# Two pairs of 64x64 products of a DeltaNet scan step, issued together over all four quadrants of the matmul array

## The chip, the cores and the metric

The kernel runs on one core of a Trainium2 chip. The metric is device time in microseconds (us) for one execution: the median of several runs, where lower is better. TensorE is called PE below, its weight loads PEld, VectorE DVE, ScalarE ACT, GpSimd POOL, and SyncE SP; SP issues nearly all DMAs.

## The reference, cut to what matters

One layer of a hybrid block: 2048 latent tokens and 256 context tokens, width 1024, all in float32. One input projection feeds two branches: neighbourhood attention (8 heads of 64, windows of 8 x 16 positions plus all context keys) and a gated DeltaNet that runs over the tokens forwards and backwards (8 heads, keys and values of 64, chunks of 64 tokens). The DeltaNet is computed chunk by chunk:

```python
def step(S, xs):
    qk_i, qd_i, kd_i, u_i, w_i, gt_i = xs
    v_new = u_i - jnp.einsum('bhck,bhkv->bhcv', w_i, S)
    o_i = jnp.einsum('bhck,bhkv->bhcv', qd_i, S) + jnp.einsum('bhij,bhjv->bhiv', qk_i, v_new)
    S = S * gt_i[..., None, None] + jnp.einsum('bhck,bhcv->bhkv', kd_i, v_new)
    return S, o_i
...
o_f, s_f = _gdn_chunked(q, k, v, g[:, :, 0], beta[:, :, 0], s0_f)
o_b, s_b = _gdn_chunked(rev(q), rev(k), rev(v), rev(g[:, :, 1]), rev(beta[:, :, 1]), s0_b)
return o_f + rev(o_b), s_f, s_b
```

Both branches are gated, projected, merged with sigmoid gates, projected once more and added to the input.

## The kernel before

**The stages.** Input projection, the DeltaNet's preparation and its triangular solves come first. Then follows a stage in which two things run woven together: the DeltaNet's scan and the attention. The output projections come last. The change touches the scan and, in three small places, the attention.

**The scan.** There are 36 steps: 4 over the context, then 32 *main* steps. A step treats one forward chunk and one backward chunk at once: direction d = 0 has partitions 0 to 63 of every tile, d = 1 has partitions 64 to 127. The state `sd` is 128 x (8 heads x 64). `scan_step` (L854) has four products, each of 16 matmuls (8 heads, 2 directions) of 64 x 64 by 64 x 64; a float32 matmul shows as two records, so a product is a batch of 32 records. Here they are called **k** (L866, keys times state, z = 0), **q** (L866, queries times state, z = 1), **p2** (L882, the chunk's solved matrix times the residual), **p4** (L889, growth of the state) and **p3** (L896, the output). That is five batches in a main step, three in a context step. Direction 0 reads and writes the lower halves of its tiles and direction 1 the upper halves, so of the array's four 64x64 quadrants the two on the diagonal are used.

The evictions: DVE multiplies k by a decay into tile `cr` (L868), subtracts that from `cv` (L871), multiplies q by the same decay into `cr` (L868 again); ACT copies p2 to `cw` (L884); DVE adds p4 to the state (L890) and subtracts p3 from the q part to give the output `co` (L898). The PSUM pool `pc` has two buffers, taken in turn.

In main steps 0 to 15 the output is stored to `os_` (L901) for the later step that treats the same chunks in the other direction. In main steps 16 to 31 the output is complete, and one step later `dn_out` (L910) normalises it: a square on ACT, a sum on DVE, a power on POOL (`ro`, L917), a product on DVE (L918), four transposes into a `pc` buffer (L922), and an eviction by DVE (`zd`, L923).

**The attention.** 32 units of 128 queries and 4 heads, handled as two pairs of heads. `scores` (L1063) and `scores_ctx` (L1063 too) form the logits; DVE adds a bias table to them (L1073) and finds the maxima (L1080, L1082); ACT takes the exponentials of the window part (L1085) and of the context part (L1088). `turn` (L1096) transposes the window part of the two heads into two tiles of the two-buffer PSUM pool `ptp`: DVE copies the first out and ACT the second (L1098, `pT`). `turn_ctx` (L1105) transposes the context part into the next `ptp` buffer, that is, the one that `turn`'s first tile held. `values` (L1116, L1120) applies the weights, `sums_inv` (`ri`, L1124 to L1128) inverts the sums, `finish` (L1133 to L1139) scales. Units at the grid's edges read the bias from the single-buffer tiles `tedge`, loaded in `att_load` (L1031); inner units read `tmid`.

**The order.** PE's order is written out by hand (`manual_schedule`, L978). The scan is a generator, and each `pump(chain, 1)` runs it to its next yield; a main step has seven yields and a unit seven pumps, so one step goes with one unit:

```python
pump(chain, 1)        # k
un.turn()
pump(chain, 1)        # q
un.turn_ctx(0)
un.scores(1)
pump(chain, 1)        # p2
...                   # scores_ctx(1), sums_inv, values(0)
pump(chain, 2)        # dn_out's transposes, then p4
un.turn()
pump(chain, 1)        # p3
un.turn_ctx(1)
...                   # scores(0) of the next unit, values(1), scores_ctx(0), finish
```

The orders of the other engines and of SP's queue are not written in the kernel: a scheduler (`schedule_with_timeline_sim`) settles them when the program is built.

One line outside this stage is of use below: L623, in the DeltaNet's preparation, multiplies keys and queries of two chunks with 64x64 matmuls in all four quadrants: first 16 records in the two quadrants that write partitions 0 to 63, then 16 in the two that write 64 to 127.

Of the kernel before, what the change touches and what calls it, by code (L numbers as in the profile page):

```python
# [8 lines left out]
F32 = mybir.dt.float32  # L9
F32R = mybir.dt.float32r  # L10
AF = mybir.ActivationFunctionType
ALU = mybir.AluOpType
# [7 lines left out]
P = 128  # L20
# [7 lines left out]
H = 8  # L28
C = 64
NCH = NT // C  # L30
CCH = TC // C
# [54 lines left out]
def body(ctx, tc, x, c, ctx_in, c_ctx, mod_w, mod_b, norm_w, w_in, conv_w, na_q_norm, na_k_norm, na_rpb,  # L86
# [99 lines left out]
    def dn_tokens(d, t0, m):  # L186
        v = d.rearrange("q (n s t) -> q n s t", s=2, t=C)
        c0, n = t0 // C, m // C
        if c0 >= 16:
            return v[:, c0 - 16:c0 - 16 + n, 0]  # L190
        return v[:, 16 - c0 - n:16 - c0, 1][:, ::-1]


    def gate_col(kind, i, p):
# [154 lines left out]
    with ExitStack() as st:  # L349
# [33 lines left out]
        for t in range(0, NTILE, 8):  # L383
            pn = bps.tile([P, 8, 64], F32, name="pn", bufs=2)
            r = range(t, min(t + 8, NTILE))
# [411 lines left out]
    with ExitStack() as st:  # L797
# [56 lines left out]
        def scan_step(i):  # L854

            main = i >= CCH
            ld = scan_in.pop(i)
            scan_load(i + 1)
            eg = egs[:, i].unsqueeze(2).to_broadcast([P, H, C])
            half = [slice(C * d, C * d + C) for d in range(2)]  # L860

            def times_state(z):
                ps = pc.tile([P, H, C], F32, name="pc")
                for h in range(H):
                    for d in range(2):
                        PE.matmul(ps[half[d], h, :], ld["ckq"][half[d], ho(h), z, :], sd[half[d], h, :], start=True, stop=True)  # L866
                t = q2.tile([P, H, C], F32, name="cr")
                V.tensor_tensor(out=t, in0=ps, in1=eg, op=ALU.mult)  # L868
                return t
            r = ld["cv"]  # L870
            V.tensor_tensor(out=r, in0=r, in1=times_state(0), op=ALU.subtract)  # L871
            yield
            if main:
                tq = times_state(1)
                if i - CCH >= 16:
                    G.tensor_tensor(out=tq.rearrange("p h e -> p (h e)"), in0=tq.rearrange("p h e -> p (h e)"), in1=os_[:, NCH - 1 - i], op=ALU.add)
                yield
            G.tensor_tensor(out=sd, in0=sd, in1=gts[:, i].unsqueeze(2).to_broadcast([P, H, C]), op=ALU.mult)  # L878
            p2 = pc.tile([P, H, C], F32, name="pc")
            for h in range(H):  # L880
                for d in range(2):
                    PE.matmul(p2[half[d], h, :], ld["cT"][half[d], ho(h), :], r[half[d], h, :], start=True, stop=True)  # L882
            w = q2.tile([P, H, C], F32, name="cw")
            S.copy(w, p2)  # L884
            yield
            p4 = pc.tile([P, H, C], F32, name="pc")
            for h in range(H):
                for d in range(2):
                    PE.matmul(p4[half[d], h, :], ld["ckd"][half[d], h, :], w[half[d], h, :], start=True, stop=True)  # L889
            V.tensor_tensor(out=sd, in0=sd, in1=p4, op=ALU.add)  # L890
            yield
            if main:
                p3 = pc.tile([P, H, C], F32, name="pc")
                for h in range(H):
                    for d in range(2):
                        PE.matmul(p3[half[d], h, :], ld["cA"][half[d], ho(h), :], w[half[d], h, :], start=True, stop=True)  # L896
                o = q2.tile([P, H, C], F32, name="co", bufs=2)
                V.tensor_tensor(out=o, in0=tq, in1=p3, op=ALU.subtract)  # L898
                if i - CCH < 16:
                    for d in range(2):  # L900
                        SP.dma_start(out=os_[half[d], i - CCH], in_=o[half[1 - d]].rearrange("p h e -> p (h e)"))  # L901
                else:
                    zd = q2.tile([P, 4, P], F32, name="zd", bufs=2)
                    SP.dma_start(out=zd, in_=d_z[1, :, :, P * (i - CCH - 16):P * (i - CCH - 15)].rearrange("p q t -> q p t"))
                    wait.append((i - CCH - 16, o, zd))
# [20 lines left out]
        def scan():  # L926

            for n in range(CCH):
                yield from scan_step(n)
            for n in range(CCH, NCH + 1):  # L930
                dn = dn_out(*wait.pop()) if wait else iter(())
                step = scan_step(n) if n < NCH else iter(())
                next(step, None)
                next(dn, None)
                yield
                for _ in range(2):
                    next(step, None)
                    yield
                next(dn, None)
                yield  # L940
                yield from step
                yield
                yield

        egs = qp.tile([P, NCH, H], F32, name="egs")
        gts = qp.tile([P, NCH, H], F32, name="gts")
        SP.dma_start(out=egs, in_=d_eg)
        SP.dma_start(out=gts, in_=d_gt)
        scan_load(0)
        chain = scan()  # L950
# [66 lines left out]
        def att_load(n):  # L1017
            hg = n // 16
            rg, cg, ty, o, r0, nr, w, br = band(n)
            if cg == 0:  # L1020
                zt = aq.tile([P, 2, 512], F32, name="azt", bufs=2)
                SP.dma_start(out=zt, in_=d_z[0, 2 * hg:2 * hg + 2, :, 512 * rg:512 * rg + 512].rearrange("p q t -> q p t"))
                rg_z[hg, rg] = zt
            if ty == 1:
                tab = [mids[hg][:, 2 * z:2 * z + 2, o:o + nr * w] for z in range(2)]
            elif edge[0] == (hg, rg, o):
                tab = edge[1]
            else:
                tab = [aq.tile([P, 2, 384], F32, name=f"tedge{z}") for z in range(2)]
                for z in range(2):  # L1030
                    SP.dma_start(out=tab[z][:, :, 0:nr * w], in_=d_tab[:, ty, 4 * hg + 2 * z:4 * hg + 2 * z + 2, o:o + nr * w])  # L1031
                edge[:] = (hg, rg, o), tab
            vt = aq.tile([P, 4, 256], F32, name="vt", bufs=2)
            for b in range(nr // br):
                a = TC + 64 * (r0 + br * b)
                SP.dma_start(out=vt[0:br * w, b, :], in_=d_nv[a:a + 64 * br, 256 * hg:256 * hg + 256].rearrange("(r c) e -> r c e", c=64)[:, KEY0[cg]:KEY0[cg] + w, :])
            return tab, vt
# [7 lines left out]
        class Unit:  # L1045
# [76 lines left out]
            def sums_inv(self):  # L1122
                ri = ap.tile([P, 4], F32, name="ri", bufs=2)
                V.tensor_tensor(out=ri, in0=self.sums[:, :, 0], in1=self.sums[:, :, 1], op=ALU.add)  # L1124
                V.tensor_scalar(out=ri, in0=ri, scalar1=2.0, scalar2=None, op0=ALU.mult)
                V.reciprocal(ri, ri)
                self.rb = ap.tile([P, 4, 64], F32, name="rb", bufs=2)
                G.tensor_copy(self.rb, ri.unsqueeze(2).to_broadcast([P, 4, 64]))  # L1128

            def finish(self):  # L1130
# [250 lines left out]
```

## Time and profile before

| what | value |
|---|---|
| median of 3 runs | 2428.86 us (2428.39 to 2434.27) |
| the profiled execution's own time | 2437.24 us |
| its span, first to last instruction | 2435.5 us |
| PE busy | 2208.8 us (91% of the span) |
| PEld busy | 1849.1 us (76%) |
| DVE busy | 1537.0 us (63%) |
| POOL busy | 1064.2 us (44%) |
| ACT busy | 779.9 us (32%) |
| DMA | 358.16 MB, mean 147 GB/s |

The profiled execution took 8.4 us more than the median of the runs; rows of the trace are times from the start of its span. PE's matmuls are pipelined, so records overlap and busy time is not work at its peak; the start of one batch to the start of the next is the better measure. "Idle before <-X" names what ended an engine's wait.

### The profile page before, as it was taken

To read this page: it belongs to the slowest core of one execution; us is meant where nothing else is said; L and a number is where in the kernel's file an instruction comes from. 1 tells how busy PE (TensorE), PEld (TensorE's weight loads), DVE (VectorE), ACT (ScalarE), POOL (GpSimd) and SP (SyncE) were. 2 spreads that over 40 slices of the span, in tenths; PEclk is the share of its full clock that TensorE was granted. 3 is DMA by queue.
4 is the path that set the end of the run, shared out by engine and by line. 5 is a ranking of instruction groups with operands and counts; after the bars stand their busy time and mean duration, and the time that the engine had idled before them with its cause. 6 is when DMAs were issued, how large, how long until landed. Compare 5 with 4: busy or idle time off the path is not lost.

```text
span 2435.5 us, 47134 instructions
## 1 busy us (share of the span) xinstructions
PE 2208.8 (91%) x18323; PEld 1849.1 (76%) x18323; DVE 1537.0 (63%) x2409; ACT 779.9 (32%) x2336; POOL 1064.2 (44%) x856
## 2 busy tenths in 40 slices
PE   6999999988888998998889987989888989899999
PEld 2778777876676787998888766777666767788998
DVE  3736877379959987849849922666566766222222
ACT  4524344211111232343554111444334444211110
POOL 2515677779865211224857510211123324643442
PEclk8999999998998999999999998999999999999999
DMA  7323444665475244254686567777886786544442
GB/s 262 106 70 81 114 118 130 156 152 121 122 173 134 64 88 115 64 131 119 181 200 176 171 153 205 211 195 196 211 216 178 184 195 177 155 118 121 113 115 89
DMA packets 461591, 358.16 MB, mean 147 GB/s; under 512 B 203253, under 2 KB 386697, under 8 KB 460809
## 3 DMA queue, kind: packets, MB, share of 16 engines
q1 hardware_dynamic: 461368, 355.16, 54.7%
q8 instruction: 144, 2.36, 0.4%
q14 instruction: 79, 0.65, 0.1%
HBM read 231.71 MB, written 119.67 MB: 144 GB/s over the span
## 4 chain that ended last, share of the span: by engine, by line
PE 44%; DVE 20%; DMA 12%; POOL 8%; issue 6%; ACT 4%; SPq 3%; DVEq 0%; POOLq 0%; ACTq 0%
PE pd L179 13%; PE pf L1351 7%; PE pu L1340 7%; DVE Xs L579 6%; DVE tmp L577 6%; PE pd L724 5%; PE pw L1063 2%; DMA tedge<-d_tab 2%; ACT pr L1085 2%; PE pc L866 1%; DMA tmk<-in_k_mk_dram 1%; POOL rn L504 1%; PE po L1116 1%; PE pt L1096 1%; DMA d_tab<-tmk 1%
## 5 line engine op out<-in xcount | busy, mean ns | idle before, releaser
L179 PE MATMUL pd<-hT,slots 128*128 128x512 f32 (+1 forms) x3360 | 825.6, 400 | 4.3 <-ACT nx L205 2.5
L179 PEld LDWEIGHTS pd<-hT,slots 128*128 128x128 f32 x3360 | 627.6, 194 | 152.6 <-issue 3.8
L577 DVE TENSOR_TENSOR tmp<-Xs 128x236 f32<-128x236 f32 (+43 forms) x310 | 337.4, 1088 | 62.4 <-DMA Xs<-d_X 54.1
L579 DVE TENSOR_TENSOR Xs<-Xs,tmp 128x236 f32<-128x236 f32 (+43 forms) x310 | 335.8, 1083 | 8.5
L125 POOL TENSOR_TENSOR slots<-w_raw,slots 128x512 fp32r<-128x512 f32 (+1 forms) x76 | 121.0, 1592 | 252.0 <-ACT slots L124 250.2
L724 PE MATMUL pd<-slots,hT 128*128 128x256 f32 x1248 | 165.5, 293 | 0.0
L724 PE MATMUL pd<-wide,hT 128*128 128x256 f32 x1248 | 158.8, 289 | 3.8 <-ACT wide L124 2.6
L724 PEld LDWEIGHTS pd<-slots,hT 128*128 128x128 f32 x1248 | 159.9, 196 | 0.0
L724 PEld LDWEIGHTS pd<-wide,hT 128*128 128x128 f32 x1248 | 155.7, 195 | 4.5 <-ACT wide L124 3.0
L878 POOL TENSOR_TENSOR sd<-sd,gts 128x512 f32<-128x512 f32 x36 | 37.6, 1045 | 238.4 <-PE pc L866 205.6
L1085 ACT ACTIVATE pr<-pr,nm 128x288 f32<-128x288 f32 (+3 forms) x128 | 77.9, 609 | 165.4 <-DVE nm L1082 165.4
L1341 DVE SCALAR_TENSOR_TENSOR gt<-gt,pu 128x256 f32<-128x256 f32 x120 | 46.3, 418 | 122.2 <-DMA gt<-d_g 76.4
L481 DVE SCALAR_TENSOR_TENSOR y<-raw,vT,y 128x512 f32<-128x512 f32 (+1 forms) x112 | 97.0, 875 | 27.5 <-ACT raw L469 22.0
L777 POOL TENSOR_TENSOR tmk<-trr,tmk 128x288 f32<-128x288 f32 (+3 forms) x72 | 98.7, 1387 | 31.0 <-DMA tmk<-in_k_mk_dram 17.3
L1342 POOL TENSOR_TENSOR gt<-gt 128x256 f32<-128x256 f32 x60 | 44.3, 739 | 127.4 <-DVE gt L1341 126.1
L1355 DVE SCALAR_TENSOR_TENSOR ckd<-pf,gate 128x512 f32<-128x512 f32 x32 | 22.0, 692 | 122.1 <-PE pf L1351 115.3
L689 POOL TENSOR_TENSOR nrn<-nss,nhalf 128x8 f32<-128x8 f32 x34 | 74.0, 2177 | 56.8 <-DVE nss L688 55.1
L205 ACT ACTIVATE zt<-pd 128x512 f32<-128x512 f32 x68 | 40.6, 597 | 180.5 <-PE pd L179 113.2
L1340 PE MATMUL pu<-ckq,OS 128*128 128x256 f32 x512 | 95.2, 284 | 2.1 <-DVE gt L1341 1.3
L124 ACT CAST slots<-w_raw 128x512 fp32r<-128x512 f32 (+1 forms) x76 | 46.6, 613 | 151.1 <-DMA w_raw<-in_w_in_dram 120.2
L866 PE MATMUL pc<-sd,ckq 64*64 64x64 f32 x2176 | 85.0, 232 | 8.5 <-DMA ckq<-d_kq 8.3
L866 PEld LDWEIGHTS pc<-sd,ckq 64*64 64x64 f32 x2176 | 75.0, 144 | 22.3 <-issue 11.3
(295 smaller groups left out, 4589.9 us busy)
## 6 DMA issues: line engine op xcount, KB each, us to landing
w_raw<-in_w_in_dram SPq DMA_DIRECT2D x92, 256.0 KB
ckq<-d_kq SPq DMA_DIRECT2D x64, 256.0 KB
gt<-d_g SPq DMA_DIRECT2D x60, 256.0 KB
d_X<-X SPq DMA_DIRECT2D x72, 128.0 KB
Xs<-d_X SPq DMA_DIRECT2D x18, 512.0 KB
d_g<-zt SPq DMA_DIRECT2D x36, 256.0 KB
cv<-d_v SPq DMA_DIRECT2D x72, 128.0 KB
cT<-d_T SPq DMA_DIRECT2D x72, 128.0 KB
```

What stands on the lines that cost most here:

```text
L125: G.tensor_tensor(out=lo[:, j:j + 4, 0:n], in0=wr, in1=hi[:, j:j + 4, 0:n].bitcast(F32), op=ALU.subtract)
L179: PE.matmul(ps[0:n, 0:m], a[:, k, 0:n], h_part(g, z, k), start=k == 0 and i == 0, stop=k == KB - 1 and i == 2)
L481: V.scalar_tensor_tensor(out=y[:, 0:m], in0=raw[:, o + j - 1:o + j - 1 + m], scalar=tap(j), in1=y[:, 0:m], op0=ALU.mult, op1=ALU.add)
L577: V.tensor_tensor(out=tv, in0=X[r, piv, cols].unsqueeze(1).to_broadcast([8 * n, m, w]), in1=X[r, rows, piv].unsqueeze(2).to_broadcast([8 * ...
L579: V.tensor_tensor(out=X[r, rows, cols], in0=X[r, rows, cols], in1=tv, op=ALU.add)
L689: G.tensor_tensor(out=rn, in0=ss, in1=nhalf, op=ALU.pow)
L724: PE.matmul(ps[:, 256 * i:256 * i + 256], h[:, 256 * j + P * i:256 * j + P * i + P], w[:, :, part, k, :], start=k == 0 and n == 0, stop=k ...
L777: G.tensor_tensor(out=mv, in0=rr[:, k0:k0 + nr, w0:w0 + n], in1=mv, op=ALU.add)
L866: PE.matmul(ps[half[d], h, :], ld["ckq"][half[d], ho(h), z, :], sd[half[d], h, :], start=True, stop=True)
L1085: S.activation(e[:, 0:nk], e[:, 0:nk], AF.Exp, bias=nm[:, u:u + 1], accum_out=self.sums[:, hh, 0:1])
L1340: PE.matmul(ps, a, r[:, k, :], start=k == 0 and n == 0, stop=k == 3 and n == 2)
L1351: PE.matmul(ps, a[:, k, P * i:P * i + P], b[k, n], start=k == 0 and m == 0, stop=k == KB - 1 and m == 2)
```

## The change

- k and q are issued together, head by head. The q product's output halves are swapped: direction 0 reads partitions 0 to 63 and writes 64 to 127, and the other way round. So the batch uses all four quadrants, with k and q in two PSUM banks. Both `pc` buffers are taken at once.
- p4 and p3 are issued together in the same way, p3 on swapped halves.
- What multiplies or follows the swapped products is laid out to match: a second decay table `egw` with swapped halves (two more DMAs of 64 partitions x 1 KB), and the token order of the gate and output tensors in DRAM (`dn_tokens`).
- In PE's order, q moves from between `turn` and `turn_ctx(0)` to k's place ahead of `turn`; p3 moves from between the second `turn` and `turn_ctx(1)` to p4's place ahead of `turn`. The count of yields stays.
- Room for `egw`: the `tedge` tiles move from pool `aq` to pool `ap`, which opens later, when the last input-projection work is done; `rb` has one buffer instead of two.

```diff
-            return v[:, c0 - 16:c0 - 16 + n, 0]
-        return v[:, 16 - c0 - n:16 - c0, 1][:, ::-1]
+            return v[:, c0 - 16:c0 - 16 + n, 1]
+        return v[:, 16 - c0 - n:16 - c0, 0][:, ::-1]
...
-            def times_state(z):
-                ps = pc.tile([P, H, C], F32, name="pc")
-                for h in range(H):
+            pss = [pc.tile([P, H, C], F32, name="pc") for _ in range(2 if main else 1)]
+            for h in range(H):
+                for z, ps in enumerate(pss):
                     for d in range(2):
-                        PE.matmul(ps[half[d], h, :], ld["ckq"][half[d], ho(h), z, :], sd[half[d], h, :], start=True, stop=True)
+                        PE.matmul(ps[half[d ^ z], h, :], ld["ckq"][half[d], ho(h), z, :], sd[half[d], h, :], start=True, stop=True)
+
+            def grown(z, e):
                 t = q2.tile([P, H, C], F32, name="cr")
-                V.tensor_tensor(out=t, in0=ps, in1=eg, op=ALU.mult)
+                V.tensor_tensor(out=t, in0=pss[z], in1=e.unsqueeze(2).to_broadcast([P, H, C]), op=ALU.mult)
                 return t
             r = ld["cv"]
-            V.tensor_tensor(out=r, in0=r, in1=times_state(0), op=ALU.subtract)
-            yield
+            V.tensor_tensor(out=r, in0=r, in1=grown(0, egs[:, i]), op=ALU.subtract)
             if main:
-                tq = times_state(1)
+                tq = grown(1, egw[:, i - CCH])
...
             p4 = pc.tile([P, H, C], F32, name="pc")
+            p3 = pc.tile([P, H, C], F32, name="pc") if main else None
             for h in range(H):
                 for d in range(2):
                     PE.matmul(p4[half[d], h, :], ld["ckd"][half[d], h, :], w[half[d], h, :], start=True, stop=True)
+                for d in range(2 if main else 0):
+                    PE.matmul(p3[half[1 - d], h, :], ld["cA"][half[d], ho(h), :], w[half[d], h, :], start=True, stop=True)
             V.tensor_tensor(out=sd, in0=sd, in1=p4, op=ALU.add)
-            yield
+            if not main:
+                yield
             if main:
-                p3 = pc.tile([P, H, C], F32, name="pc")
-                for h in range(H):
-                    for d in range(2):
-                        PE.matmul(p3[half[d], h, :], ld["cA"][half[d], ho(h), :], w[half[d], h, :], start=True, stop=True)
...
+        egw = qp.tile([P, NCH - CCH, H], F32, name="egw")
         SP.dma_start(out=egs, in_=d_eg)
+        for d in range(2):
+            SP.dma_start(out=egw[C * d:C * d + C], in_=d_eg[C - C * d:P - C * d, CCH:])
...
-                tab = [aq.tile([P, 2, 384], F32, name=f"tedge{z}") for z in range(2)]
+                tab = [ap.tile([P, 2, 384], F32, name=f"tedge{z}") for z in range(2)]
...
-                self.rb = ap.tile([P, 4, 64], F32, name="rb", bufs=2)
+                self.rb = ap.tile([P, 4, 64], F32, name="rb")
```

## Rows read from the trace of the kernel before

**Rows 1.** Stage of scan and attention: us, PE, PEld, DVE, ACT, POOL busy, clock, DMA.

```profile
1505.00:2056.00 551.00, 486.84 (x8021) 389.80 (x8020) 363.94 (x945) 237.94 (x698) 141.17 (x140) 0.96 0.76 195
```

**Rows 2.** Chain that ended last, this stage, shares by line.

```profile
by line: PE pw L1063 10.6%; DMA tedge<-d_tab 7.4%; ACT pr L1085 7.3%; PE pc L866 5.9%; PE po L1116 5.2%; PE pt L1096 5.1%; issue 5.0%; DVE mx L1080 4.8%; PE pt L1105 4.2%; PE pc L882 4.1%; DMA d_oz<-azt 2.9%; PE po L1120 2.7%; ACT pr L1088 
```

**Rows 3.** The same chain in order of time: start, us, what.

```profile
1508.17 1.08 PE pc L866 x32
...
1645.72 1.08 PE pc L896 x32
...
2019.12 1.15 PE pc L896 x32
...
2026.80 1.08 PE pc L866 x32
```

**Rows 4.** Timeline of PE in one unit (start, us, instruction, idle before).

```profile
1637.50 1.12 PE L1096 MATMUL pt<-ident,pr 128*120 128x128 f32 x6 [0.51 <-ACT pr L1085]
1638.55 1.15 PE L866 MATMUL pc<-sd,ckq 64*64 64x64 f32 x32
1639.63 0.66 PE L1105 MATMUL pt<-ident,pr 128*128 128x128 f32 x4
...
1646.73 0.66 PE L1105 MATMUL pt<-ident,pr 128*128 128x128 f32 x4
```

**Rows 5.** Timeline of DVE in the same unit.

```profile
1638.30 0.55 DVE L1098 COPY pT<-pt 120x384 f32<-120x384 f32 x1
...
1645.64 0.55 DVE L1098 COPY pT<-pt 120x384 f32<-120x384 f32 x1
```

**Rows 6.** Timeline of a unit with 512 window columns.

```profile
1607.47 0.68 DVE L1098 COPY pT<-pt 128x512 f32<-128x512 f32 x1
...
1608.45 0.66 PE L1105 MATMUL pt<-ident,pr 128*128 128x128 f32 x4
```

**Rows 7.** Matmuls (x, with those in flight) of L623 in 0.26 us.

```profile
470.80:471.06 0.26, 0.26 (x24) 0.26 (x19) 1.00 0.00 0
```

**Rows 8.** The same of L866.

```profile
1621.01:1621.27 0.26, 0.26 (x16) 0.26 (x13) 1.00 1.04 244
```

**Rows 9.** Waits in this stage: us in total, times, longest.

```profile
DVE ri L1124 <- ACT pr L1088: 43.8, 20, 2.5
...
DVE co L918 <- POOL ro L917: 6.6, 11, 1.4
...
PE pc L896 <- DVE zd L923: 5.5, 7, 1.0
```

**Rows 10.** Timeline of a unit of the second half, PE and DVE.

```profile
1801.95 1.15 PE L889 MATMUL pc<-cw,ckd 64*64 64x64 f32 x32
1803.03 0.88 PE L1096 MATMUL pt<-ident,pr 128*128 128x128 f32 x6
1804.62 1.15 PE L896 MATMUL pc<-cw,cA 64*64 64x64 f32 x32 [0.71 <-DVE zd L923]
1805.70 0.66 PE L1105 MATMUL pt<-ident,pr 128*128 128x128 f32 x4
...
1803.35 0.16 DVE L1124 TENSOR_TENSOR ri<-sums 128x4 f32<-128x4 f32 x1 [2.28 <-ACT pr L1088]
...
1803.84 0.72 DVE L923 SCALAR_TENSOR_TENSOR zd<-pc,vT,zd 128x512 f32<-128x512 f32 x1
```

**Rows 11.** Another such unit.

```profile
1906.16 0.75 DVE L923 SCALAR_TENSOR_TENSOR zd<-pc,vT,zd 128x512 f32<-128x512 f32 x1 [0.89 <-PE pc L922]
...
1909.01 0.66 PE L1105 MATMUL pt<-ident,pr 128*128 128x128 f32 x4
```

**Rows 12.** Start of the attention, SP and DVE.

```profile
1473.83 0.66 SPq L1031 DMA_DIRECT2D tedge<-d_tab  x1
...
1496.25 0.37 SPq L958 DMA_DIRECT2D fwr<-d_nq  x1
...
1503.61 0.46 DVE L1073 CUSTOM_DVE_ANT_0 pr<-pw,tedge 128x288 f32<-128x288 f32 x1 [13.34 <-PE pw L1063]
```

More of the change, by code (lines that the diff above doesn't have):

```diff
@@ L858, in scan_step @@
             scan_load(i + 1)
-            eg = egs[:, i].unsqueeze(2).to_broadcast([P, H, C])
             half = [slice(C * d, C * d + C) for d in range(2)]
-            def times_state(z):
-                ps = pc.tile([P, H, C], F32, name="pc")
-                for h in range(H):
+            pss = [pc.tile([P, H, C], F32, name="pc") for _ in range(2 if main else 1)]
+            for h in range(H):
+                for z, ps in enumerate(pss):
                     for d in range(2):
-                        PE.matmul(ps[half[d], h, :], ld["ckq"][half[d], ho(h), z, :], sd[half[d], h, :], start=True, stop=True)
+                        PE.matmul(ps[half[d ^ z], h, :], ld["ckq"][half[d], ho(h), z, :], sd[half[d], h, :], start=True, stop=True)
+            def grown(z, e):
                 t = q2.tile([P, H, C], F32, name="cr")
-                V.tensor_tensor(out=t, in0=ps, in1=eg, op=ALU.mult)
+                V.tensor_tensor(out=t, in0=pss[z], in1=e.unsqueeze(2).to_broadcast([P, H, C]), op=ALU.mult)
                 return t
             r = ld["cv"]
-            V.tensor_tensor(out=r, in0=r, in1=times_state(0), op=ALU.subtract)
-            yield
+            V.tensor_tensor(out=r, in0=r, in1=grown(0, egs[:, i]), op=ALU.subtract)
             if main:
-                tq = times_state(1)
+                tq = grown(1, egw[:, i - CCH])
                 if i - CCH >= 16:
@@ L889, in scan_step @@
                     PE.matmul(p4[half[d], h, :], ld["ckd"][half[d], h, :], w[half[d], h, :], start=True, stop=True)
+                for d in range(2 if main else 0):
+                    PE.matmul(p3[half[1 - d], h, :], ld["cA"][half[d], ho(h), :], w[half[d], h, :], start=True, stop=True)
             V.tensor_tensor(out=sd, in0=sd, in1=p4, op=ALU.add)
-            yield
+            if not main:
+                yield
             if main:
-                p3 = pc.tile([P, H, C], F32, name="pc")
-                for h in range(H):
-                    for d in range(2):
-                        PE.matmul(p3[half[d], h, :], ld["cA"][half[d], ho(h), :], w[half[d], h, :], start=True, stop=True)
                 o = q2.tile([P, H, C], F32, name="co", bufs=2)
@@ L943, in scan @@
                 yield
+                yield
         egs = qp.tile([P, NCH, H], F32, name="egs")
         gts = qp.tile([P, NCH, H], F32, name="gts")
+        egw = qp.tile([P, NCH - CCH, H], F32, name="egw")
         SP.dma_start(out=egs, in_=d_eg)
+        for d in range(2):
+            SP.dma_start(out=egw[C * d:C * d + C], in_=d_eg[C - C * d:P - C * d, CCH:])
         SP.dma_start(out=gts, in_=d_gt)
```

## The prediction

> **What bounds the kernel now.** I read the page first: PE is busy through nearly the whole span. The change touches the stage in which scan and attention run together, so next come the busy times of that stage: 551 us, of which PE has 487, DVE 364, ACT 238, POOL 141, and the DMA engines are busy for 0.76 of it [rows 1]. The reader is to see that PE has 64 us to spare and DVE 187: neither is full, so what counts is the chain, not the sum of the work. The chain of the stage goes by turns through PE (logits, values, transposes, scan), DVE (maxima), ACT (exponentials) and loads of the bias table [rows 2]. The scan's k and q line has 5.9% of it, some 32 us, though all its batches together would be 64 x 1.08 = 69 us. In order of time the chain holds 25 q batches (first and last: the L866 rows), each right behind the transposes of L1096 and ahead of those of L1105, and 10 p3 batches (first and last: the L896 rows), 9 of them in the second half [rows 3]. The k batches are hardly on it: in the unit shown PE ends k and waits 0.51 us for ACT's exponential [rows 4]. So merging q into k can take at most 25 x 1.08 = 27 us off the chain, and p3 into p4 at most 11 us. The question is what comes next in line where they stood.
>
> **Do four quadrants overlap?** The batches now use two. L623 uses all four. In a 0.26 us stretch in which its first half still runs and its second half begins, 24 matmuls are in flight or start [rows 7]; in an equal stretch of L866 it is 16 [rows 8]. Both are at full clock and of the same shape. So the second pair of quadrants runs beside the first, and I cost a merged batch of 64 records at 1.08 us, the price of one batch today. The other bound is 2.16 us, no overlap at all. The Trainium skill (TensorE: Matmul & The Clock Gate, "Wait — 56ns, not 53.3ns?") has a rule against this: starts of matmuls never come closer than about 25 ns, which would make 64 records 1.6 us, an estimate by that page. The trace disagrees: a batch of 32 in 1.08 us is 34 ns a start, and 24 against 16 makes that some 22 ns.
>
> **q out of the gap between L1096 and L1105.** The transposes of L1105 go into the `ptp` buffer that the first `pT` copy empties. That copy ends at 1638.30 + 0.55 = 1638.85; with some 0.05 us for the signal, L1105 starts at 1638.90 in place of 1639.63 [rows 4, 5]: 0.73 us, not 1.08. In a unit with 512 window columns the copy ends at 1607.47 + 0.68 = 1608.15, and L1105 started at 1608.45 [rows 6]: 0.25 us. Of the 25 units, 6 are of this kind: 19 x 0.73 + 6 x 0.25 = 15.4 us. This supposes that DVE does the copy where it does it now, right behind k's product. The bounds: 27 us if the copy moves forward, and a loss if it moves back (a rival below). In its new place q is free: it runs inside k's 1.08 us, and even past that the 0.51 us wait covers it.
>
> The Trainium skill says the same in general (TensorEngine Tiling (Array Packing), "PSUM Bottleneck": after tiling, the copy out of PSUM may become the limit). By PE's time alone 64 batches less would be 69 us; by the copy it is 15; the 0.25 us left in the wide unit agrees with that page.
>
> **p3 ahead of the second turn, first half.** p3 is on the chain in 1 of 16 units there. In 20 of the 32 units DVE stands at `ri` waiting for ACT's last exponential (43.8 us in all) [rows 9], and the copy that L1105 waits for is queued behind it; p3 lay in that wait and costs nothing now. Where DVE doesn't stand, the copy ended at 1645.64 + 0.55 = 1646.19 and L1105 started at 1646.73 [rows 4, 5]: up to 0.5 us, in some 6 units. Against it, p3 is ready sooner, and if its subtraction (0.68 us, as a copy of that size in [rows 6]) goes ahead of the copy, some 10 units lose that. I take 0, with -3 and +7 us as ends.
>
> **p3 behind `zd`, second half.** This is the new wait. The transposes of `dn_out` use the `pc` buffer that p3 needs next, so p3 waits for DVE's `zd`. Today only p3 waits, behind p4 and the second turn. Merged, the third matmul of the p4/p3 batch waits, and behind it in PE's queue stand p4's rest, the second `turn` and L1105. In 7 of the 16 units p3 waits for `zd` already [rows 9], because DVE stands at `ri` ahead of it. In such a unit p4 could start at 1801.95; `zd` ends at 1803.84 + 0.72 = 1804.56. Merged, the batch ends at 1804.62 + 1.08 = 1805.70, the state's addition takes 0.68, the copy 0.55, L1105 starts near 1807.0 in place of 1805.70 [rows 10]: +1.3 us. Where `zd` is on time, it ends at 1906.16 + 0.75 = 1906.91, the batch at 1908.05, addition and copy at 1909.28; L1105 at 1909.3 in place of 1909.01 [rows 11]: +0.3. So 7 x 1.3 + 9 x 0.3 = 11.8 us. Not all is paid: in 11 of these units DVE later waits for POOL's `ro`, 6.6 us in all [rows 9], and `ro` hangs on p3's output, which comes no later than now; a unit that is late elsewhere waits less there. I take 11.8 - 6.6 = +5.2, with +1 and +18 as ends (18: 14 late units of 1.3).
>
> **The bias table in the later pool.** The first `tedge` load was issued 30 us ahead of its use [rows 12]. In `ap` it must wait until the projection work is done, as the query load (`fwr`) does, issued at 1496.25. Then 2 x 295 KB more travel in front of the first logits; at the 195 GB/s of this stage [rows 1] that is 3.0 us. Ends: 0 (lands in time) and 7.4 us (a whole query load's way to first use again, 1496.25 to 1503.61). I take +3. Later loads are single-buffered before and after; nothing changes. `egw`'s two DMAs lie far ahead of their use, between loads that are prefetched; `rb`'s one buffer was read at the end of the unit before; `dn_tokens` moves the same bytes. Each 0; uncovered, an SP issue is some 0.5 us [rows 12].
>
> **Sum.** -15.4 + 0 + 5.2 + 3 = -7.2 us. The profiled execution took 2437.24 us, 8.4 above the median; the same difference on the median gives 2428.86 - 7.2 = 2421.7. About 0.3% (7.3 us) is what a measurement of this kernel can tell from no change, so the forecast stands at that edge. Its own range, from double to half the q term, is 2406 to 2430.
>
> **Rivals.** *The chain shortens by the whole batches.* If the scheduler's new order puts the copies early and DVE's waits at `ri` shrink, 25 + 10 batches of 1.08 us come off: -38 + 3 = -35, 2394 us. For it: all of these are on the chain [rows 3]. Against it: the copies [rows 5, 6] are right behind.
>
> *Slower: DVE takes q's product ahead of the copy.* k's product, the residual's subtraction and q's product now become ready together, ahead of the turn. If subtraction and q's product go first, the copy ends 2 x 0.68 later and L1105 starts 0.63 later than today (0.43 in wide units). One operation ahead (0.68) is the point from which the gain of 0.73 is gone; two decide for a loss. DVE's total is unchanged, so some of the delay is caught up: between 0 and 14.6 us, I take 8. Then +8 + 5.2 + 3 = +16, 2445 us. For it: in the wide unit the copy came only after the subtraction. Against it: in the other unit it came first.
>
> *Nothing.* Bias loads and `d_oz` stores have 10.3% of the chain [rows 2], with single buffers whose loads are as long as ever; units that wait for them give the gain back: 2429 us.
>
> *The quadrants don't overlap*, or by half only: the p4/p3 batch costs up to 1.08 us more ahead of the second turn. k with q would end 0.6 us past the wait. By the 9 second-half units with p3 on the chain this is +10, the q term falls to about -3: 2444 us. By the page's 25 ns it would be half of that. Against it: [rows 7, 8].
>
> **How the numbers follow.** Forecast 0.42, whole batches 0.16, DVE's order 0.24, nothing 0.14, no overlap 0.04. Half of the forecast's chance lies beyond the edge. Faster: 0.21 + 0.16 + 0.02 (of nothing) = 0.39. Slower: 0.22 + 0.03 + 0.01 = 0.26. Same: the rest, 0.35. The range reaches from 2396, near the whole batches, to 2446, just past the second rival.
>
> **What would show it.** Right: batches of 64 records of some 1.1 us; L1105 starting right behind the first copy and PE waiting there for DVE; more PE waiting for `zd`, at the head of the merged p4/p3 batch in the second half; first logits some us later. Wrong: batches of 2 us; q's product ahead of the copy on DVE; a copy that is no longer what L1105 waits for; a lower granted clock, as PE does less in the same time (0.96 now [rows 1]).

## The result and the profile after

The changed kernel takes 2447.91 us (median of 6 runs, 2441.09 to 2452.54), against 2434.9 us for the kernel before in the same comparison: ratio 1.0056 [1.0041, 1.0071]. It is 0.56% slower, some 13.6 us, where 7.2 us less were forecast. The profiled execution is the fastest of the six, 2441.09 us, so its rows show only part of the loss.

The stage of scan and attention, over the same stretch as [rows 1], same columns:

```profile
1505.00:2056.00 551.00, 428.48 (x7976) 332.45 (x7980) 358.96 (x942) 236.43 (x694) 145.84 (x138) 0.93 0.75 194
```

PE's busy time fell by 58 us, from 487 to 428, and the stage is not shorter. PE's waits in the stretch (us in total, times, longest), with the rows on DVE's waits that answer to [rows 9] below them:

```profile
PE pt L1112 <- DVE pT L1105: 29.5, 31, 2.5
PE pt L1103 <- ACT pr L1092: 22.2, 30, 1.7
PE pt L1112 <- ACT pT L1105: 18.7, 21, 1.9
PE pw L1070 <- DVE mx L1080: 16.3, 4, 5.8
PE pc L895 <- DVE zd L926: 16.0, 15, 2.6
PE pt L1112 <- ACT ob L915: 9.6, 2, 8.5
...
DVE ri L1131 <- ACT pr L1095: 54.5, 30, 2.5
...
DVE co L921 <- POOL ro L920: 7.4, 12, 1.8
```

All ten rows of PE's waits add up to 121 us; before, six rows made 63. The 58 us taken from PE came back as 58 us of waiting: 37 more for the copies ahead of `turn_ctx` (L1112, was L1105), 10 more for `zd` ahead of p3 (L895, was L896), and 9.6 in two waits of `turn_ctx` that the profile puts down to ACT's `ob`, one of them 8.5 us long; step 26 below shows what it is. The copies' row before the change, over the same stretch:

```profile
PE pt L1105 <- DVE pT L1098: 11.4, 14, 1.5
```

The unit of [rows 4, 5], now:

```profile
1636.98 1.16 PE L866 MATMUL pc<-sd,ckq 64*64 64x64 f32 x64
1638.65 1.12 PE L1103 MATMUL pt<-ident,pr 128*120 128x128 f32 x6 [0.50 <-ACT pr L1092]
1640.14 0.63 PE L1112 MATMUL pt<-ident,pr 128*128 128x128 f32 x4 [0.37 <-ACT pr L1095]
...
1638.84 0.68 DVE L870 TENSOR_TENSOR cr<-pc,egs 128x512 f32<-128x512 f32 x1
1639.44 0.55 DVE L1105 COPY pT<-pt 120x384 f32<-120x384 f32 x1
1639.91 0.68 DVE L873 TENSOR_TENSOR cv<-cv,cr 128x512 f32<-128x512 f32 x1
1640.62 0.69 DVE L870 TENSOR_TENSOR cr<-pc,egw 128x512 f32<-128x512 f32 x1
```

The batch of 64 records takes 1.16 us, and 32 took 1.15 [rows 4]: the second pair of quadrants adds nothing that can be seen. From the first turn to `turn_ctx` it is now 1.49 us, before 2.13 [rows 4], and DVE takes the copy first, the subtraction (L873) and q's product later.

A unit of the second half shows what the merged p4/p3 batch does. PE, then DVE:

```profile
1851.45 0.33 PE L893 MATMUL pc<-cw,ckd 64*64 64x64 f32 x4
1854.22 0.27 PE L895 MATMUL pc<-cw,cA 64*64 64x64 f32 x2 [2.44 <-DVE zd L926]
...
1855.30 1.20 PE L1103 MATMUL pt<-ident,pr 128*120 128x128 f32 x6
1857.31 1.09 PE L1112 MATMUL pt<-ident,pr 128*128 128x128 f32 x4 [0.80 <-DVE pT L1105]
1858.32 0.79 PE L1070 MATMUL pw<-KH,qh 64*128 64x512 f32 x2
...
1852.90 0.16 DVE L1131 TENSOR_TENSOR ri<-sums 128x4 f32<-128x4 f32 x1 [2.24 <-ACT pr L1095]
...
1853.42 0.75 DVE L926 SCALAR_TENSOR_TENSOR zd<-pc,vT,zd 128x512 f32<-128x512 f32 x1
1855.40 0.69 DVE L896 TENSOR_TENSOR sd<-sd,pc 128x512 f32<-128x512 f32 x1 [1.24 <-PE pc L895]
1856.01 0.68 DVE L901 TENSOR_TENSOR co<-cr,pc 128x512 f32<-128x512 f32 x1
1856.61 0.55 DVE L1105 COPY pT<-pt 120x384 f32<-120x384 f32 x1
```

Four records of p4 run; then a record of p3 waits 2.44 us for `zd`, and the other 28 of p4 stand behind it. Only after that come the state's addition, the output's subtraction and the copy, in a row on DVE, and `turn_ctx` is 5.86 us behind p4's first record. DVE has this order in all 16 steps of the second half; before, the copy stood ahead of the output's subtraction in every step.

### The profile page after: what moved, and what is told of

The parts are those of the page before. It is cut to its first block, busy times and chain, and to the rows that moved or that the text cites. A ratio compares the mean times of both kernels' runs of the same rounds, so it can differ in the third digit from the quotient of the medians.

```text
span 2439.3 us, 47115 instructions
## 1 busy us (share of the span) xinstructions
PE 2156.0 (88%) x18323; PEld 1795.4 (74%) x18323; DVE 1538.2 (63%) x2409; ACT 780.0 (32%) x2336; POOL 1070.0 (44%) x856
## 4 chain that ended last, share of the span: by engine, by line
PE 38%; DVE 25%; DMA 13%; POOL 8%; issue 7%; ACT 5%; SPq 4%; DVEq 0%; POOLq 0%; ACTq 0%
PE pd L179 9%; DVE Xs L579 7%; DVE tmp L577 7%; PE pf L1358 7%; PE pu L1347 7%; PE pd L724 5%; PE pw L1070 2%; DMA tmk<-in_k_mk_dram 1%; DMA d_v<-xT 1%; POOL rn L504 1%; DMA tedge<-d_tab 1%; DVE mx L1087 1%; PE po L1123 1%; ACT pr L1092 1%; DMA w_raw<-in_w_in_dram 1%
## 5 line engine op out<-in xcount | busy, mean ns | idle before, releaser
L880 POOL TENSOR_TENSOR sd<-sd,gts 128x512 f32<-128x512 f32 x36 | 44.4, 1233 | 166.3 <-PE pc L866 97.3
L481 DVE SCALAR_TENSOR_TENSOR y<-raw,vT,y 128x512 f32<-128x512 f32 (+1 forms) x112 | 96.2, 867 | 27.5 <-ACT raw L469 22.1
L1135 POOL COPY rb<-ri 128x256 f32<-128x256 f32 x32 | 12.8, 401 | 198.2 <-DVE ri L1133 198.2
L1112 PE MATMUL pt<-ident,pr 128*128 128x128 f32 x256 | 42.4, 290 | 61.4 <-DVE pT L1105 30.7
```

The source lines that it names most:

```text
L481: V.scalar_tensor_tensor(out=y[:, 0:m], in0=raw[:, o + j - 1:o + j - 1 + m], scalar=tap(j), in1=y[:, 0:m], op0=ALU.mult, op1=ALU.add)
```

## Where the steps spend their time

From the first records of the batches the trace gives the mean length of each part of a scan step. The table is worked out from them (us a step, 16 steps a row; half 1 is steps 0 to 15; the last step has no next k, and `step` is the sum of the parts):

```
                     k->turn  ->turn_ctx  ->p4  ->turn 2  ->turn_ctx 2  ->next k   step
before         half 1  1.69      2.17     4.75    1.11        2.45        4.41    16.58
               half 2  2.14      2.46     5.32    1.08        2.62        4.26    17.88
layout         half 1  1.69      2.18     4.67    1.11        2.48        4.34    16.46
               half 2  2.16      2.38     5.44    1.09        2.59        4.24    17.90
changed        half 1  1.70      1.79     4.69    1.09        2.33        4.70    16.30
               half 2  2.11      1.59     5.83    2.46        2.39        4.03    18.42
q_only         half 1  1.70      2.13     4.58    1.08        2.56        4.15    16.20
               half 2  2.42      1.84     5.88    1.13        2.54        4.11    17.92
p3_only        half 2  1.91      2.25     5.34    3.16        2.14        4.21    19.02
p3_first_half  half 2  2.61      1.77     6.12    1.12        2.65        4.13    18.39
zd_early       half 2  2.27      1.71     5.63    1.19        2.33        4.57    17.70
serial_p       half 2  2.12      1.49     5.82    2.26        1.61        3.89    17.18
serial_p_late  half 2  2.17      1.52     5.66    2.14        1.66        3.68    16.83
```

In the changed kernel q's place gave 0.38 and 0.87 us a step, 20 us in all. In the second half 0.51 of it came back at once, between `turn_ctx` and p4, and the way from p4 to the second `turn` grew by 1.38.

These means hide where the second half's loss stands. From k to the next k, over the 15 steps that have one (us, worked out from the same records):

```
                  step 26  step 29  the other 13
before              17.7     18.6      232.2
q_only              15.6     19.0      231.9
changed             27.9     24.9      221.7
  repeated          29.0     23.7      223.5
zd_early            22.9     23.9      220.8
serial_p            16.6     21.9      221.0
serial_p_late       18.1     21.8      211.3
p3_only             19.8     20.9      243.9
zd_early_p3_only    17.1     18.6      236.2
serial_p3_only      16.8     17.5      236.0
```

In the changed kernel steps 26 and 29 are 16.5 us longer than before, and the other 13 together 10.5 us shorter. In both steps a load is late. Step 26, PE, ACT, DVE, and then step 29, DVE and PE:

```profile
1956.67 1.09 PE L1103 MATMUL pt<-ident,pr 128*128 128x128 f32 x8
1966.31 1.09 PE L1112 MATMUL pt<-ident,pr 128*128 128x128 f32 x4 [8.55 <-ACT ob L915]
...
1963.30 0.62 ACT L1199 CAST OS<-fwr 128x512 fp32r<-128x512 f32 x1 [7.34 <-DMA fwr<-in_w_o_dn_dram]
...
1963.95 0.42 DVE L1202 TENSOR_TENSOR KL<-fwr,OS 128x256 fp32r<-128x256 f32 x1 [7.53 <-ACT OS L1199]
1964.29 0.68 DVE L896 TENSOR_TENSOR sd<-sd,pc 128x512 f32<-128x512 f32 x1
...
2013.42 0.56 DVE L1080 CUSTOM_DVE_ANT_0 pr<-pw,tedge 128x384 f32<-128x384 f32 x1 [6.08 <-DMA tedge<-d_tab]
...
2014.04 0.58 PE L1070 MATMUL pw<-KHc,qh 64*128 64x256 f32 x1 [5.70 <-DVE mx L1080]
```

In step 26 ACT and DVE stand for a block of the output projection's weights (`fwr`), whose conversion the scheduler put ahead of the state's addition and the copies; PE waits 8.55 us behind them. The conversion (L1195, now L1202) stood ahead of the addition before the change too, at 1963.12 against 1963.67, but there ACT and DVE didn't wait for the block:

```profile
1961.48 1.13 ACT L1192 CAST OS<-fwr 128x512 fp32r<-128x512 f32 x2
```

In step 29 DVE waits for the bias table; before, it didn't in that step. Over the second half DVE's waits for the table are 11.7 us, before 5.5. The 0.51 us between `turn_ctx` and p4 is this: without steps 26 and 29 that part is 5.34 us, before 5.30. No run takes these two waits away alone, so whether the loads are late because the units come sooner, or because the scheduler ordered the queues anew, isn't shown.

## The experiments

All ratios are to the kernel before, measured beside each version. The changed kernel repeated gave 2450.49 us, 1.0052 [1.0039, 1.0066].

> The changed kernel itself, to have its time and a second profile beside the parts on one chip. Expected: +10 to +17 us against the kernel before, its span's scan and attention stage some 4 to 12 us later at the end.

**The parts one by one.** `layout` keeps the swapped halves, `egw`, `tedge` in the later pool and the one `rb` buffer, with all five batches in their old places. `q_only` adds the merged k/q to it, `p3_only` the merged p4/p3.

```diff
 # q apart (layout, p3_only)
+            product(0)
...
             if main:
+                yield
+                product(1)
                 tq = grown(1, egw[:, i - CCH])
 # p3 apart (layout, q_only)
             V.tensor_tensor(out=sd, in0=sd, in1=p4, op=ALU.add)
+            yield
+            if main:
+                p3 = pc.tile([P, H, C], F32, name="pc")
...
```

> Only the layout: outputs on swapped halves, the second decay table, the bias tiles in the later pool and one rb buffer; all five batches stand where they stood before. Theory 1 (the loss is p3's new place, ahead of the second turn and behind zd): 0 to +5 us against the kernel before, all of it at the attention's start. Theory 2 (the loss is the layout, that is, the later load of the bias table and a new order of SP's queue): +10 us or more. Theory 3 (less work lets the granted clock fall): 0, and a clock as before.

> The layout and the merged k and q; p3 stays in a batch of its own between the second turn and turn_ctx. Theory 1: faster than the layout alone by 8 to 15 us, so -10 to -3 us against the kernel before. Theory 2: as slow as the changed kernel. Theory 3: half of the changed kernel's loss, +5 us, with a clock between the two.

> The layout and the merged p4 and p3; q stays in a batch of its own between the first turn and turn_ctx. Theory 1: slower than the layout alone by 8 to 18 us, so +10 to +22 us against the kernel before. Theory 2: as slow as the changed kernel. Theory 3: half of the changed kernel's loss, +5 us.

Measured: 1.0004 [0.9993, 1.0016], 1.0005 [0.9994, 1.0015] and 1.0098 [1.0082, 1.0114]. The layout costs nothing that can be told, k/q alone brings nothing, p4/p3 alone costs 23 us; for `q_only` 3 to 10 us less than before had been expected. PE's waits for `zd` between 1770 and 2070 us are 5.4 us in `layout` and 22.8 in `p3_only`.

A unit of `q_only` in the first half shows why the gap doesn't shorten there (PE, then DVE):

```profile
1670.71 1.36 PE L1104 MATMUL pt<-ident,pr 128*128 128x128 f32 x8 [0.63 <-ACT pr L1093]
1673.07 0.63 PE L1113 MATMUL pt<-ident,pr 128*128 128x128 f32 x4 [0.99 <-DVE pT L1106]
...
1671.50 0.82 DVE L873 TENSOR_TENSOR cv<-cv,cr 128x512 f32<-128x512 f32 x1
1672.24 0.68 DVE L1106 COPY pT<-pt 128x512 f32<-128x512 f32 x1
```

The subtraction stands ahead of the copy here. That is so in 24 of the 32 units of `q_only`, in 6 before, in 13 of the changed kernel. In the changed kernel the first `turn` to `turn_ctx` takes 1.41 us with the copy first and 2.11 with the subtraction first (before: 2.26 and 2.60). In the first half of `q_only` the gap is 2.13 us, in `layout` 2.18. In its second half the gap does shorten, from 2.38 to 1.84, though the subtraction goes first in 11 of 16 units, and the step is no shorter (17.92 against 17.90): the gain is gone between `turn_ctx` and p4 (5.88 against 5.44) and ahead of the first `turn` (2.42 against 2.16). Why stays open.

**One half at a time.** The merged p4/p3 in steps 0 to 15 alone, or 16 to 31 alone, with k/q merged in both:

```diff
+            early = main and (i - CCH < 16)      # or >= 16
-                for d in range(2 if main else 0):
+                for d in range(2 if early else 0):
```

> The changed kernel, but p3 is merged with p4 only in main steps 0 to 15, where no zd stands ahead of it; in steps 16 to 31 p3 is a batch of its own in its old place. Theory 1 (the loss is the wait for zd at the head of the merged batch, second half only): -6 to +2 us against the kernel before. Rival (p3 ahead of the second turn costs in every step, since nothing covers DVE's copy any more): half of the loss, about +6 us.

> The opposite: p3 merged with p4 only in main steps 16 to 31. Theory 1: all of the loss, +10 to +16 us against the kernel before. Rival: about +6 us.

Measured: 1.0045 [1.0032, 1.0057] and 1.0073 [1.0056, 1.0089]. The second lost more than expected (18 us), with 22.1 us of PE's waits for `zd` and only 17.3 us in step 26, so there is a loss without the long wait of step 26. The first was not expected. Its first half, with p4/p3 merged, takes 16.58 us a step, 16.20 in `q_only`. Its second half runs the code of `q_only` and takes 18.39 us a step against 17.92, with the same waits for `zd` (6.7 and 5.8 us). The subtraction stands ahead of the copy in 15 of its 16 steps there, against 11 of 16, but the gap behind it is no longer (1.77 us against 1.84). That difference stays open.

**`zd` earlier, output later.** `zd_early` runs `dn_out`'s transposes and `zd` between the first `turn` and `turn_ctx`, long before p3. `late_o` issues the output's subtraction behind the second `turn`.

```diff
 # zd_early
                 next(step, None)
                 next(dn, None)
                 yield
-                for _ in range(2):
-                    next(step, None)
-                    yield
+                next(step, None)
                 next(dn, None)
                 yield
+                next(step, None)
+                yield
+                yield
```

> The changed kernel with dn_out's transposes and zd moved from right ahead of the merged p4/p3 batch to the yield between the first turn and turn_ctx, two batches earlier. Theory 1: p3 finds its buffer free, PE's waits for zd (16 us in the second half) are gone, -8 to +3 us against the kernel before. Rival: as slow as the changed kernel, +10 us or more.

> The changed kernel with DVE's subtraction of p3 issued after the second turn, so that the copy of turn's first tile stands ahead of it in program order. If the copy behind the subtraction costs (theory of the second turn's order): 3 to 8 us less than the changed kernel, +5 to +10 us against the kernel before. If only zd counts: as the changed kernel, +12 us.

Measured: 1.0009 [0.9996, 1.0022] and 1.0059 [1.0043, 1.0075]. With the waits for `zd` gone (16.0 us to 0.7) nearly all of the loss is gone. That the waits were the loss is not shown by this alone: the 13 other steps take 220.8 us, as in the changed kernel (221.7), and of the 11 us won some 5 are step 26's (22.9 us, 27.9 in the changed kernel). `late_o` tested nothing: the scheduler put DVE's operations in the same order as before it (state, output, copy in every step of the second half that the trace holds), so it is one more run of the changed kernel.

**Is early `zd` a gain by itself?** The same move on the other three versions:

> Layout with the five batches in the old places, and dn_out's transposes and zd brought forward to between the first turn and turn_ctx. This is the control for zd_early. If early zd is only worth something where p3 stands behind zd (my theory), there is at most the 5.4 us of PE's waits for zd in layout to win: ratio to before 0.998 to 1.001. If early zd is a gain by itself, whatever the batches, it is near the 11 to 12 us that zd_early had over the changed kernel: ratio 0.995 to 0.997.

> p3_only (merged p4/p3, k and q apart) with zd early. p3_only is at 1.0098 with 22.8 us of PE's waits for zd in the second half. Theory that these waits are the loss: they fall under 3 us and the ratio to 0.999 to 1.003. Rival, that the loss is a lower granted clock or other things that go with the merged p4/p3 batch: ratio 1.006 or more, also with the waits gone.

> q_only (merged k/q, p3 in its old place) with zd early. Theory: like layout against zd_early_layout, q merged is worth nothing to some us: 0.997 to 1.001. If it stands over 0.3 per cent below zd_early, merged p4/p3 costs also with its zd wait gone; if it is level with zd_early, that wait was all that merged p4/p3 cost.

Measured: 1.0032 [1.0019, 1.0045], 1.0035 [1.0023, 1.0048], 1.0018 [1.0003, 1.0033]. Where p3 is in its old place, early `zd` costs 0.28% (`layout`) and, with intervals that overlap, 0.13% (`q_only`); where p4/p3 is merged it gains 0.63% and 0.47%. All three lie above what was expected, `p3_only` with early `zd` just so. For `p3_only` step 26 is no great part of it (19.8 us and 17.1), so there the gain belongs to the merged batch and its wait. The cost of early `zd` in `q_only` stands in steps 26 and 29, 28.1 and 25.4 us against 15.6 and 19.0; its other 13 steps are 14 us shorter.

**Same places, no overlap.** `after_serial` issues all of k, then all of q; all of p4, then all of p3.

```diff
-            for h in range(H):
-                for z, ps in enumerate(pss):
+            for z, ps in enumerate(pss):
+                for h in range(H):
...
-                for d in range(2 if main else 0):
+            for h in range(H if main else 0):
+                for d in range(2):
...
```

> The changed kernel with all batches in their new places, but issued so that the quadrants hardly overlap: all of k's 32 records, then all of q's; all of p4's, then all of p3's. Tells what the overlap is worth apart from the places. If PE's time is what counts there, 1.08 us of q (less the 0.37 to 0.66 us that PE waits for the pT copy behind the batch anyway) and 1.08 us of p3 in each of 32 steps come on top: 48 us at most, ratio 1.018 to 1.026. If PE's saved time is given back anyway, in waits or in clock, the ratio is 1.006 to 1.012. If the overlap is worth nothing: 1.005.

Measured: 0.9983 [0.9971, 0.9995]. No theory had it faster than the changed kernel; it is faster than before, too. k and q together take 1.91 us there in most steps, interleaved 1.16. So the new places, without the overlap, cost nothing. Two theories were left: p3's records held p4's (T), or overlap gives its time back through the clock (O). `serial_p` takes the second hunk of the diff alone, `serial_q` the first, `zd_early_serial` both with early `zd`, `serial_p_late` the second hunk in steps 16 to 31 alone.

> The changed kernel with k and q still on all four quadrants together, but p4's 32 records all ahead of p3's 32 at the same place. Theory T: what cost in the change is that p3's records, which wait for the buffer that zd frees, stand between p4's, so that p4 and the chain through sd wait too; p4's batch ahead covers that wait. Then ratio 0.995 to 1.000, PE's waits for zd in the second half from 16 us to under 4. Theory O: overlapping batches give their time back by the clock, whichever batch it is: 1.001 to 1.004.

> The changed kernel with k's 32 records all ahead of q's 32, and p4 and p3 still interleaved. Theory T: the waits for zd stay at about 16 us and the loss stays, 1.005 to 1.010. Theory O: half of the way to after_serial, 1.000 to 1.004.

> after_serial with zd early. Theory T: after_serial has no wait for zd left to win (1.6 us once), so early zd brings nothing and may cost what it cost layout (1.0004 to 1.0032): 0.998 to 1.002. If early zd is a gain beside the order of the records: 0.996 or less.

> The changed kernel with p4 ahead of p3 in steps 16 to 31 alone, where zd is in play; in steps 0 to 15 all four quadrants together. Theory T: first half as the changed kernel (243 to 249 us), second half as after_serial (274 us to 280): 0.995 to 0.999, at or under serial_p. Theory O, or merged p3 in the first half setting off the loss in the second as it did with q merged (second half 294 us): 1.002 to 1.005.

Measured: **`serial_p` 0.9941 [0.9920, 0.9963], `serial_p_late` 0.9939 [0.9921, 0.9958]**, `serial_q` 1.0043 [1.0028, 1.0058], `zd_early_serial` 1.0050 [1.0034, 1.0066]. The order of the records decides: p4 ahead of p3 turns 0.56% slower into 0.59% faster, 28 us, a little more than T's range. Beside q in its old place the same order (`serial_p3_only` below, 1.0053, against `p3_only`, 1.0098) wins 11 us. That it works as T says is shown in part. The waits for `zd` do shrink, but of those 28 us 14 stand in steps 26 and 29 (16.6 and 21.9 us, 27.9 and 24.9 in the changed kernel), and the other 13 steps are the same (221.0 and 221.7; 211.3 in `serial_p_late`). With q in its old place these 13 steps do gain, 243.9 to 236.0 us.

k ahead of q alone (1.0043 against 1.0056, intervals that overlap) hardly helps, and it missed both ranges: its waits for `zd` fell to 8.7 us, where T had them stay. With p4 ahead of p3, k and q interleaved are worth 0.42% (`after_serial` to `serial_p`), with intervals that don't overlap, so the overlap does pay there. `zd_early_serial` missed its range on the slow side; its step 26 takes 31.0 us, 17.0 in `after_serial`, which is most of the difference of 16 us. A unit of `serial_p` like the one above (PE, then DVE):

```profile
1856.03 1.15 PE L893 MATMUL pc<-cw,ckd 64*64 64x64 f32 x32
1858.81 1.15 PE L896 MATMUL pc<-cw,cA 64*64 64x64 f32 x32 [1.63 <-DVE zd L927]
1859.88 0.87 PE L1104 MATMUL pt<-ident,pr 128*120 128x128 f32 x6
1861.38 0.66 PE L1113 MATMUL pt<-ident,pr 128*128 128x128 f32 x4 [0.62 <-ACT pT L1106]
...
1858.66 0.68 DVE L897 TENSOR_TENSOR sd<-sd,pc 128x512 f32<-128x512 f32 x1
1860.07 0.69 DVE L902 TENSOR_TENSOR co<-cr,pc 128x512 f32<-128x512 f32 x1 [0.73 <-PE pc L896]
1860.67 0.55 DVE L1106 COPY pT<-pt 120x384 f32<-120x384 f32 x1
```

p4's batch fills part of the wait for `zd`, and the second `turn` still comes 3.85 us behind p4's first record, as above. But DVE adds p4 to the state while p3 runs, so the copy is earlier: `turn_ctx` is 5.35 us behind p4's first record, not 5.86. Over the second half `turn_ctx` is 3.87 us behind p4 in `serial_p`, 4.85 in the changed kernel: 0.20 of that is won ahead of the second `turn`, 0.78 behind it. In most steps of `serial_p` p3 doesn't wait at all: PE's waits for `zd` are 3.3 us in 2 steps, against 16.0 in 15.

**Two last questions.** `serial_p3_only` is `serial_p` with q back in its old place; `serial_p_sd_behind` issues the state's addition behind the output's subtraction:

```diff
                 V.tensor_tensor(out=o, in0=tq, in1=p3, op=ALU.subtract)
+                V.tensor_tensor(out=sd, in0=sd, in1=p4, op=ALU.add)
```

> serial_p with k and q apart again, q's batch in its old place between the first turn and turn_ctx. Between layout and q_only merging k and q was worth nothing (1.0004 and 1.0005). If that holds where p3 stands behind p4 too, the ratio is that of serial_p, 0.992 to 0.996. If the forecast's term of 15.4 us for q comes out here, it is 0.999 to 1.002.

> serial_p with DVE's addition to sd behind the subtraction of p3 and no longer ahead of it. Theory A: part of what serial_p won is that this addition (0.69 us) lies in the time of p3's batch; behind it, it stands ahead of DVE's copy of pT and the second turn_ctx, 0.6 us in each of 16 to 32 steps, 10 to 19 us: ratio 0.998 to 1.002. Theory B: what serial_p won is that PE's pause is cut in two parts, and the granted clock stays at its upper level behind it (1.00 against 0.54 in one unit); then the addition's place matters little: 0.993 to 0.996.

Measured: 1.0053 [1.0040, 1.0065] and 0.9950 [0.9934, 0.9967]. q's place is worth 1.1%, some 27 us, beside p4 ahead of p3, which was outside of both ranges. The other run tested nothing: the scheduler put the addition ahead of the subtraction again.

## Why the prediction was wrong

**Quadrants overlap:** right, 1.16 us for 64 records.

**The layout:** +3 us forecast, 1 us by `layout`; the first bias addition came at 1505.54 us, before at 1503.61 [rows 12].

**p3 ahead of the second turn, first half:** right within its ends. Without a wait for `zd` the part from p4 to the second `turn_ctx` is 3.42 us in half 1, before 3.56, but the part behind it grew from 4.41 to 4.70: 2.4 us in all over 16 steps (6 in the changed kernel repeated), where 0 was taken and +7 was the end.

**q out of the gap:** the step failed. The 0.73 us were there, and the 20 us between `turn` and `turn_ctx` are more than the 15.4 forecast. But the term took a shorter gap for a shorter step. Measured in time, q merged is worth 0 beside the old p3 (1.0004 to 1.0005), 10 us beside the interleaved p3 (1.0098 to 1.0056) and 27 us beside p4 ahead of p3 (1.0053 to 0.9941). Some 8 us of what the second lacks are the late load of step 26, which takes 19.8 us in `p3_only` and 27.9 in the changed kernel. `q_only` shows half of the slower rival: not q's product but the subtraction went ahead of the copy, in 24 of 32 units. One operation ahead was named as the point from which the gain is gone; in the first half it was (2.13 us, in `layout` 2.18), in the second the gap shortened all the same.

**Later loads:** the step that failed outright. "Later loads are single-buffered before and after; nothing changes" stands at 0 in the sum. Measured, DVE's waits for the table in the second half went from 5.5 to 11.7 us, and the weight block of step 26, which the forecast doesn't name, held PE for 8.55 us. Steps 26 and 29 are 16.5 us longer, the other 13 are 10.5 us shorter, so in these profiles the two steps are more than the whole loss of the second half. The rival *Nothing* had the mechanism: units that wait for single-buffered loads give the gain back. What made the loads late stays open.

**p3 behind `zd`:** the mechanism was right, the size wrong. +11.8 less 6.6 was forecast. Between p4 and the second `turn_ctx` 3.70 us became 4.85, 1.15 a step or 18.4 us, of which 6.7 are step 26's. 15 steps waited, not 7: p4's batch and the second turn had covered `zd` in the others, and the merged batch reaches p3 after a few records. The sum put only the state's addition and the copy behind the batch; DVE takes the output's subtraction between them in all 16 steps, 0.60 us in the unit shown. That some 12 us are left without step 26, next to the 11.8 reckoned, is luck. The credit was wrong: DVE's waits for `ro`, counted as cover, are 7.4 us after, 6.6 before. Added to `q_only`, the merged p4/p3 of both halves costs 0.51%, 12.4 us against 0 + 5.2 forecast, late loads included. With 0.2 for q and 1.0 for the layout that makes the 13.6 us measured.

**What stays open:** how much of the loss the changed kernel would have without the late loads, why q alone gains nothing in the second half of `q_only`, and how much of the gain of `serial_p` over the changed kernel is the order of p4 and p3, how much DVE's addition, and how much the loads. The scheduler settles DVE's order anew for every version, and the parts don't add up.

## What to carry to other kernels

Two batches may be issued together without being interleaved: if one of them waits for a buffer, put all records of the one that doesn't wait first, or it inherits the wait. Don't put later loads at nothing because their buffers stay as they were: a unit that comes sooner may wait for them. Before costing a removed batch, look at which operation of the next engine frees what comes after it, and whether a scheduler may reorder that engine. When PE loses 58 us of work and the stage doesn't shrink, add up its waits before and after: they name the new bound. Look at the longest single wait too: a mean over 16 steps hid one of 8.55 us.

## What the hardware showed beyond that

In the unit of the changed kernel PE pauses for 2.44 us ahead of p3; the granted clock falls behind that, in the second turn (1.00 from 1855.30 to 1855.60, 0.66 and 0.50 in the two stretches of 0.3 us after it), and ahead of the pause of 0.80 us. In that of `serial_p`, with pauses of 1.63 and 0.62 us, it doesn't fall. Both stretches below begin about when `turn_ctx` does; first the changed kernel, then `serial_p` (the clock is the third column from the end):

```profile
1857.30:1863.00 5.70, 5.69 (x37) 4.16 (x38) 2.77 (x7) 1.01 (x3) 1.65 (x1) 0.54 0.65 197
```

```profile
1861.30:1865.00 3.70, 3.62 (x38) 2.60 (x38) 2.63 (x7) 1.14 (x3) 1.65 (x1) 1.00 1.00 247
```

0.54 is close to all of the stretch at 1.2 GHz, and the transposes of `turn_ctx` take 1.09 us there against 0.66. Over the stage the clock is 0.96 before, 0.93 changed and 0.94 in `serial_p`, so over the whole stage the clock hardly tells the last two apart. No run here set the clock alone.
